# Eight experts, 67 MB of weights: float32 loads in the hardware queue and a cast on VectorE in place of casting loads from Pool

## The chip, the core and the metric

The kernel runs on one core of a Trainium2 chip. The core has five engines with queues of their own: TensorE (PE; PEld is its weight load), VectorE (DVE), ScalarE (ACT), GpSimd (POOL) and SyncE (SP), and 16 DMA engines that all of them share. The metric is device time in microseconds, the median of several runs, lower is better.

## What is computed

Eight independent experts, each with two matrix products and a ReLU between them. All arrays are float32.

```python
n_experts, capacity, hidden, expert_hidden = 8, 256, 512, 2048

def reference(x, w1, w2):          # x 8x256x512, w1 8x512x2048, w2 8x2048x512
    h = np.matmul(x, w1)
    h = np.maximum(h, 0)
    return np.matmul(h, w2).astype(np.float32)
```

Each of the 16 weight matrices has 4.194 MB (4 MiB) and is used once; x and the output have 4.194 MB each.

## The kernel before

Everything is multiplied in bf16 and accumulated in float32. x is loaded whole, 32 KB for each of 128 partitions, in two transfers (`HEAD`), cast to bf16 by VectorE and ScalarE, and transposed by TensorE into `xT`, in four rounds of 2 x 16 small matmuls, whose results VectorE and ScalarE copy out of PSUM (line 237).

Then a loop over the experts runs on TensorE. The first layer of an expert is 64 matmuls (`xT` against `w1_sb`), in two halves of two groups of 16; after each group ScalarE applies the ReLU and writes `hT` (line 279). The second layer is 32 matmuls (`hT` against `w2_sb`) into two PSUM banks `o_ps`, one for each 128 rows of output; VectorE copies both into `out_sb` (line 263), and for the last expert ScalarE copies the second one (line 285). All matmuls have line 315 in the profile, since one helper records them.

The weights come by casting DMAs that Pool issues (line 227): they read float32 from memory and write bf16 into one of `NS = 4` slots of `w1_sb` and `w2_sb`. The list `loads` sets their order: w1 and w2 of experts 0 and 1 together, then of 2 and 3, then w1 of 4 and 5, and from there mostly one matrix at a time; the last w2 is cut in two (`CUT`). Pool issues a load for a slot as soon as TensorE has read that slot's old contents, so several loads stand in its queue at any time. SyncE waits for the loads in the same order (line 179) and tells TensorE through the semaphores `c_w1` and `c_w2`; a whole w2 counts as two halves. SyncE's own queue carries x, the store of experts 0 to 6 in one transfer (line 174), issued when their outputs are in `out_sb`, and the store of expert 7 (line 186). The two queues feed the same 16 DMA engines.

Of the kernel before, what the change touches and what calls it, by code (L numbers as in the profile page):

```python
# [8 lines left out]
FP32 = mybir.dt.float32  # L9
BF16 = mybir.dt.bfloat16  # L10
# [6 lines left out]
def kernel(  # L17
# [7 lines left out]
    nc = tc.nc  # L25
    P = 128
# [7 lines left out]

    HEAD = 4

    NS = 4


    GJ = 4  # L40
    UG = 2
    NG = K2 // GJ

    JH = K2 // 2
    CUT = 11

    x_v = x.rearrange("e (pp r) k -> (e pp) (r k)", r=R)  # L50
    w1_v = w1.rearrange("e (p ko) n -> p e (ko n)", ko=K1)
    w2_v = w2.rearrange("e (p j) n -> p e j n", j=K2)
# [21 lines left out]
    x_sb = w2_sb[:, 2, :]  # L74
    X_AT = W2_AT + 2 * K2 * H * 2
# [14 lines left out]
    d_w = {  # L90
        (w, i): sem(f"d_w{w}_{i}")
        for w, slots in [(1, (0, 2, 3)), (2, (0, 1, 2, 3))]
        for i in slots
    }
    d_x, d_half = [sem(f"d_x{i}") for i in range(2)], sem("d_half")
    s_event, s_cast, s_stored = sem("s_event"), sem("s_cast"), sem("s_stored")
    s_pe, v_last = sem("s_pe"), sem("v_last")

    def take(engine, s, n):
        engine.wait_ge(s, n).then_inc(s, -n)  # L100
# [16 lines left out]

    loads = []  # L120
    for es in [(0, 1), (2, 3)]:
        loads += [(1, es, 0, 1), (2, es, 0, K2)]
    loads += [(1, (4, 5), 0, 1), (2, (4,), 0, K2), (2, (5,), 0, K2)]
    for e in range(6, E - 1):
        loads += [(1, (e,), 0, 1), (2, (e,), 0, K2)]
    loads += [(1, (E - 1,), 0, 1), (2, (E - 1,), 0, CUT), (2, (E - 1,), CUT, K2)]
    landed, counts = [], {}
    for w, es, a, _ in loads:
        s = d_half if a else d_w[w, es[0] % NS]
        counts[id(s)] = counts.get(id(s), 0) + 16  # L130
        landed.append((s, counts[id(s)]))

# [14 lines left out]

    sp = nc.sync

    def wide(a):  # L150
        rows, run = list(a.ap)
        return mybir.PhysicalAccessPattern(
            ap=[rows, [run[1], 1], run],
            offset=a.offset,
            dtype=a.dtype,
            memref=a.memref,
            memsetref=a.memsetref,
            dynamic_ap_info=a.dynamic_ap_info,
            shape_register=a.shape_register,
            bass_ap=a.bass_ap,  # L160
        )

    def copy_rows(dst, src):

        inst = mybir.InstDMACopy(
            name=nc.get_next_instruction_name(),
            engine=mybir.EngineType.SP,
            ins=[wide(a) for a in sp.lower_ap_dma(src)],
            outs=sp.lower_ap_dma(dst),
            mode="Copy",  # L170
            cce_op=mybir.AluOpType.bypass,
            queue="qSPDynamicHW",
        )
        return sp.add_instruction(inst)

    for i, (w, es, a, b) in enumerate(loads):
        sp.wait_ge(*landed[i])
        halves = 2 if b - a == K2 else 1
        sp.sem_inc((c_w1, c_w2)[w - 1], halves * len(es))
        if i == len(loads) - 2:  # L180
            sp.wait_ge(s_event, 3)
            copy_rows(
                out_v[:, :E - 1, :], out_sb[:, :E - 1].rearrange("p e m h -> p (e m h)")
            ).then_inc(d_last, 16)
    sp.wait_ge(v_last, MC)
    sp.dma_start(
# [4 lines left out]


    pool = nc.gpsimd

    def build_identity():
        pool.memset(identity[:], 0.0).then_inc(s_event)  # L196
        pool.wait_ge(s_event, 1)

        pool.affine_select(  # L199
            out=identity[:],  # L200
            in_=identity[:],
            compare_op=mybir.AluOpType.not_equal,
            fill=1.0,
            base=0,
            pattern=[[-1, P]],
            channel_multiplier=1,
        ).then_inc(s_event)

    for i, (w, es, a, b) in enumerate(loads):


        old = es[-1] - NS
        if w == 2 and 2 in es:
            build_identity()
            pool.wait_ge(*after_transposes(K1 * MC))
        if old >= 0 and a == 0:
            if w == 1:
                pool.wait_ge(*after_hidden(old, NG))
            else:
                pool.wait_ge(*after_outputs(old, MC))  # L220
        e, ne, at_slot = es[0], len(es), es[0] % NS
        if w == 2:
            src = w2_v[:, e:e + ne, a:b, :].rearrange("p e j n -> p e (j n)")
            dst = w2_sb[:, at_slot:at_slot + ne, a * H:b * H]
        else:
            src, dst = w1_v[:, e:e + ne, :], w1_sb[:, at_slot:at_slot + ne, :]
        pool.dma_start(dst, src).then_inc(landed[i][0], 16)  # L227
    pool.wait_ge(s_stored, 1)
    used = [s.num for s in sems[1:]]
    used = range(min(used), max(used) + 1)  # L230
# [9 lines left out]
        )  # L240


    dve = nc.vector
    SPLIT = 12

    def cast(copy, a, b):
        return copy(x_sb[:, rows(a, b)], x_f32[:, rows(a, b)])  # L247

    dve.wait_ge(d_x[0], 16)
    cast(dve.tensor_copy, 0, HEAD).then_inc(s_cast)  # L250
    dve.wait_ge(d_x[1], 16)
    cast(dve.tensor_copy, HEAD, SPLIT).then_inc(s_cast)
    dve.sem_inc(c_xt[0], 1)
    for ko in range(K1):
        dve.wait_ge(*after_transposes(ko * MC + 1))
        copy_xt(dve.tensor_copy, ko, 0).then_inc(c_xt[0])
    dve.sem_inc(c_o, MC)
    for e in range(E):
        for m in range(MC):
            if e == E - 1 and m == 1:  # L260
                break
            dve.wait_ge(*after_outputs(e, m + 1))
            cp = dve.tensor_copy(out_sb[:, e, m, :], o_ps[m][:])  # L263
            cp.then_inc(v_last if e == E - 1 else c_o)
        if e == E - 2:
            dve.drain().then_inc(s_event)


    act = nc.scalar
    act.wait_ge(d_x[1], 16)  # L270
    cast(act.copy, SPLIT, R).then_inc(s_cast)
    act.sem_inc(c_xt[1], 1)
    for ko in range(K1):
        act.wait_ge(*after_transposes(ko * MC + 2))
        copy_xt(act.copy, ko, 1).then_inc(c_xt[1])
    for e in range(E):
        for g in range(NG):
            act.wait_ge(*after_hidden(e, g + 1))
# [5 lines left out]
    act.wait_ge(*after_outputs(E - 1, MC))  # L284
    act.copy(out_sb[:, E - 1, 1, :], o_ps[1][:]).then_inc(v_last)  # L285

# [46 lines left out]
    def last_column(step):  # L333

        return (P - 1) * step * 2
# [5 lines left out]
    def transposes():  # L341
        i = 0
        for m in range(MC):
            take(pe, c_xt[m], 1)
            for r2 in range(R // MC):
                if i % 6 == 0:
                    for k in range(i, min(i + 6, n)):
                        row = (k % (R // MC)) * MC + k // (R // MC)
                        pe.reg_add(bank[i // 6 % 2][k - i], reg["x"], row * H * 2)
                    if i + 6 > n:  # L350
                        pe.reg_add(reg["x"], reg["x"], 2)
                t = matmul(
                    xt_ps[m][:, r2, :],
                    at(w2_sb, bank[i // 6 % 2][i % 6], [[K1, P]]),
                    pe.lower_ap(identity[:]),
                    start_tensor_calc=True,
                    stop_tensor_calc=True,
                    is_transpose=True,
                )
                i += 1  # L360
            t.then_inc(s_pe)

    pe.wait_ge(s_event, 2)
    pe.wait_ge(s_cast, 3)
    x_first = X_AT + last_column(K1)
    pe.reg_mov(reg["x"], x_first)
# [36 lines left out]
        compute(address1, range(a, b), regs)  # L403

    def set_expert():
        slot = reg["slot"]
        pe.reg_mod(slot, count, NS)
        pe.reg_mul(slot, slot, K1 * F * 2)
        pe.reg_add(reg["b1"], slot, W1_AT + last_column(K2))
        pe.reg_add(reg["b2"], slot, W2_AT)  # L410
        for ko in range(K1):
            pe.reg_add(reg[f"xt{ko}"], reg[f"xt{ko}"], P * 2)
        first_addresses()
# [100 lines left out]
```

## Time and profile before

| What | Value |
|---|---|
| median of 3 runs | 179.04 us (179.0 to 179.16) |
| the profiled execution | 179.38 us |
| its span, first to last instruction | 178.1 us |
| TensorE busy | 127.6 us, 72% |
| ScalarE busy | 40.6 us, 23% |
| VectorE busy | 18.1 us, 10% |
| Pool's DMA queue, share of 16 engines | 88.7% |
| SyncE's DMA queue, share of 16 engines | 11.3% |

An engine's busy time is what its instructions took; a DMA queue's share is the time of its packets against 16 engines over the span. The MB of a queue are the bytes it wrote, so a casting load of float32 into bf16 counts half of what it read. What stands outside the span (1.3 us of the profiled execution) is start and end of the program.

### The profile page before, as it was taken

The page shows a single profiled execution, that of the slowest core. Times are in us where ns is not written, and L with a number is a line of the kernel's source. Part 1 is how long each engine was busy: PE and PEld are TensorE (multiplying, and loading weights), DVE is VectorE, ACT ScalarE, POOL GpSimd, SP SyncE. Part 2 cuts the span into 40 slices and gives each one's busy share as a digit, 9 for nine tenths or more (in the row PEclk, how much of TensorE's full clock was granted, in tenths as well). Part 3 has the DMA queues.
Part 4 walks back from the last instruction along what each step waited for, and adds up shares of the span by engine and source line. Part 5 has one row for each costly group of instructions (what it writes and reads, how often), then busy time and mean ns, then how long its engine had stood idle before and what let it go on. Part 6 is the DMA issues. An engine that isn't in the chain of part 4 may idle for free. (4 is left out here: it accounts for less than half of the span.)

```text
span 178.1 us, 2074 instructions
## 1 busy us (share of the span) xinstructions
PE 127.6 (72%) x832; PEld 89.5 (50%) x832; DVE 18.1 (10%) x21; ACT 40.6 (23%) x39; POOL 9.2 (5%) x18
## 2 busy tenths in 40 slices
PE   0000066698039999994069999999999999969980
PEld 0000055587014695593023695596597498449530
DVE  0200435200000200200000200200020020020010
ACT  2000424226000053044000063044044036005310
POOL 3500000100000002101000101110000000000000
PEclk9999999999957999999756999999999999999996
DMA  6999999999999989989989999999999999999997
GB/s 212 431 294 300 236 213 199 236 217 195 236 202 210 236 177 236 232 180 236 232 180 236 232 195 221 232 202 213 236 202 210 236 210 202 236 198 202 336 412 324
DMA packets 2945, 41.94 MB, mean 236 GB/s; under 512 B 257, under 2 KB 257, under 8 KB 513
## 3 DMA queue, kind: packets, MB, share of 16 engines
q0 software_dynamic: 2368, 33.56, 88.7%
q1 hardware_dynamic: 576, 8.39, 11.3%
q14 instruction: 1, 0.00, 0.0%
HBM read 71.30 MB, written 4.19 MB: 424 GB/s over the span
## 5 line engine op out<-in xcount | busy, mean ns | idle before, releaser
L315 PE MATMUL o_ps<-w_sb,hT 128*128 x256 | 61.4, 402 | 16.8 <-PEq L100 16.8
L315 PE MATMUL h_ps<-xT,w_sb 128*128 x512 | 60.2, 279 | 3.2 <-PEq L100 3.2
L315 PEld LDWEIGHTS h_ps<-xT,w_sb 128*128 x512 | 57.3, 145 | 7.0 <-issue 3.9
L279 ACT ACTIVATE hT<-h_ps 128x1024 bf16<-128x1024 f32 x32 | 32.7, 1023 | 100.3 <-PE h_ps L315 100.3
L315 PEld LDWEIGHTS o_ps<-w_sb,hT 128*128 128x128 bf16 x256 | 25.6, 102 | 49.9 <-issue 23.8
L315 PE MATMUL xt_ps<-identity,w_sb 128*128 128x128 bf16 x64 | 7.6, 310 | 25.3 <-PEq L100 25.3
L263 DVE COPY out_sb<-o_ps 128x512 f32<-128x512 f32 x15 | 9.7, 686 | 130.4 <-PE o_ps L315 130.4
L315 PEld LDWEIGHTS xt_ps<-identity,w_sb 128*128 x64 | 6.5, 144 | 26.0 <-issue 26.0
L227 POOL DMA_DIRECT2D w_sb<-in_w_dram x12 | 7.4, 621 | 106.5 <-PE h_ps L315 47.5
L237 ACT COPY xT<-xt_ps 128x1024 bf16<-128x1024 bf16 x4 | 4.0, 1012 | 7.7 <-PE xt_ps L315 7.7
L247 ACT CAST w_sb<-out_sb 128x2048 bf16<-128x2048 f32 x1 | 1.9, 1898 | 16.5 <-DMA out_sb<-in_x_dram 16.5
L237 DVE COPY xT<-xt_ps 128x1024 bf16<-128x1024 bf16 x4 | 4.9, 1224 | 5.8 <-PE xt_ps L315 5.8
L247 DVE CAST w_sb<-out_sb 128x2048 bf16<-128x2048 f32 (+1 forms) x2 | 3.5, 1760 | 19.0 <-DMA out_sb<-in_x_dram 19.0
L285 ACT COPY out_sb<-o_ps 128x512 f32<-128x512 f32 x1 | 0.6, 585 | 5.9 <-PE o_ps L315 5.9
L247 ACT ACT_TABLE_LOAD x1 | 1.3, 1283 | 2.4 <-PEq L146 2.4
L199 POOL TENSOR_SCALAR_AFFINE_SELECT identity<-identity 128x128 bf16<-128x128 bf16 x1 | 1.4, 1375 | 0.2 <-POOL identity L196 0.2
L196 POOL MEMSET identity<- 128x128 bf16 x1 | 0.2, 231 | 0.0
L498 POOL MEMSET const-float32-0.0<- 128x1 f32 x1 | 0.1, 98 | 0.2 <-issue 0.2
L498 POOL MEMSET const-bfloat16-1.0<- 128x1 bf16 x1 | 0.1, 101 | 0.0
L498 POOL MEMSET const-uint8-127<- 128x1 uint8 x1 | 0.1, 101 | 0.0
L498 POOL MEMSET const-float32-1.0<- 128x1 f32 x1 | 0.1, 98 | 0.0
## 6 DMA issues: line engine op xcount, KB each, us to landing
w_sb<-in_w_dram POOLq DMA_DIRECT2D x5, 4096.0 KB, 47.8
w_sb<-in_w_dram POOLq DMA_DIRECT2D x5, 2048.0 KB, 50.7
out_dram<-out_sb SPq DMA_DIRECT2D x1, 3584.0 KB, 11.6
out_sb<-in_x_dram SPq DMA_DIRECT2D x1, 3072.0 KB, 19.0
w_sb<-in_w_dram POOLq DMA_DIRECT2D x1, 1408.0 KB, 50.0
out_sb<-in_x_dram SPq DMA_DIRECT2D x1, 1024.0 KB, 4.8
w_sb<-in_w_dram POOLq DMA_DIRECT2D x1, 640.0 KB, 52.5
out_dram<-out_sb SPq DMA_DIRECT2D x1, 512.0 KB, 4.5
```

What stands on the lines that cost most here:

```text
L196: pool.memset(identity[:], 0.0).then_inc(s_event)
L199: pool.affine_select(out=identity[:], in_=identity[:], compare_op=mybir.AluOpType.not_equal, fill=1.0, base=0, pattern=[[-1, P]], channel_ ...
L227: pool.dma_start(dst, src).then_inc(landed[i][0], 16)
L237: return copy(xT[:, ko, m].rearrange("k (ep r2) -> k ep r2", r2=R // MC), xt_ps[m][:].rearrange("k r2 ep -> k ep r2"),)
L247: return copy(x_sb[:, rows(a, b)], x_f32[:, rows(a, b)])
L263: cp = dve.tensor_copy(out_sb[:, e, m, :], o_ps[m][:])
L279: act.activation(hT[:, g * GJ:(g + 1) * GJ, :].rearrange("p a c -> p (a c)"), h_ps[g % UG][:], mybir.ActivationFunctionType.Relu,).then_in ...
L285: act.copy(out_sb[:, E - 1, 1, :], o_ps[1][:]).then_inc(v_last)
L315: return pe.add_instruction(inst)
L498: nc = _bacc.Bacc("TRN2", target_bir_lowering=False, num_devices=1)
```

## The change

All loads go through SyncE's hardware queue, in float32, into a staging buffer `stage` with two places: one for w1, one for w2. VectorE casts from there into a single bf16 copy, `w1_sb` or `w2_sb`. A w1 is cast in one instruction of 8192 columns, a w2 in two of 4096. SyncE issues w1 and w2 of expert 0 right behind x; after that, a matrix of the next expert is issued when the cast of the same matrix of this expert is done, so that at most one transfer stands behind the running one. VectorE starts a cast when the load has landed and TensorE has read the old bf16 copy. The output copies and the xT copies that VectorE made move to ScalarE, except one of the last expert.

For the last expert w1 comes in two transfers (three quarters and one quarter), and ScalarE casts about a third of it beside VectorE; w2 comes in two halves. The store of experts 0 to 6 stands in the same queue behind the last load. Pool is left with the identity matrix. The order on TensorE stays as it was; only its address arithmetic loses the slots, since there is one copy to read.

```diff
-    NS = 4
+    NS = 2
...
-    w1_sb = allot("w1_sb", [P, NS, K1 * F], BF16)
-    w2_sb = allot("w2_sb", [P, NS, K2 * H], BF16)
+    stage = allot("stage", [P, NS, K1 * F], FP32)
+    w1_sb = allot("w1_sb", [P, K1 * F], BF16)
+    w2_sb = allot("w2_sb", [P, K2 * H], BF16)
...
+    KEEP = K1 - 1
+    LATE = F // 8 * 5
...
+    issue_all(1, 0)
+    issue_all(2, 0)
+    for i, (w, e, a, b) in enumerate(loads):
+        for k in range(len(casts[i])):
+            sp.wait_ge(s_weights, last_cast[i] - len(casts[i]) + k + 1)
+            if w == 2 or b == K1 * F:
+                sp.sem_inc((c_w1, c_w2)[w - 1], 1)
+        if b == K1 * F:
+            issue_all(w, e + 1)
+        if (w, e) == (1, E - 1) and b == K1 * F:
+            sp.wait_ge(s_out, 1)
+            copy(
...
+    for i, (w, e, a, b) in enumerate(loads):
+        dve.wait_ge(*landed[i])
+        if a == 0:
+            if (w, e) == (2, 0):
+                dve.wait_ge(*after_transposes(K1 * MC))
+            if e > 0:
+                dve.wait_ge(*(after_hidden(e - 1, NG) if w == 1 else after_outputs(e - 1, MC)))
+        helped = w == 1 and e == E - 1
+        for a, b in casts[i]:
+            if helped:
+                b = b - F if b < K1 * F else a + LATE
+                cast_w(dve.tensor_copy, i, a, b)
+                dve.wait_ge(s_helped, 1 if a == 0 else 2)
+                dve.drain().then_inc(s_weights)
+            else:
+                cast_w(dve.tensor_copy, i, a, b).then_inc(s_weights)
...
+        if e == E - 2:
+            for i, (w, e1, a, b) in enumerate(loads):
+                if (w, e1) == (1, E - 1):
+                    act.wait_ge(*landed[i])
+                    if a == 0:
+                        act.wait_ge(*after_hidden(e, NG))
+                    cast_w(act.copy, i, b - F if a == 0 else a + LATE, b).then_inc(s_helped)
+        for m in range(MC):
+            act.wait_ge(*after_outputs(e, m + 1))
+            if e < E - 1:
+                act.copy(out_sb[:, e, m, :], o_ps[m][:]).then_inc(c_o)
```

SyncE's queue before, the whole of it. The first two rows load x, the last two store the output; the waits of the store name the loads' semaphores, since SyncE passes their landings on to TensorE first.

```order
L143 DMA out_sb_55<-in_x_dram 128x2048
L143 DMA out_sb_55<-in_x_dram 128x6144
L146 UNCONDITIONAL_BRANCH
L174 DMA out_0_dram<-out_sb_55 128x7x1024 [waits barrier_Pool_Activation_PE_DVE_SP_release,d_w1_0,d_w2_0,d_w1_2,d_w2_2,d_w2_1,d_w1_3,d_w2_3,s_event]
L186 DMA out_0_dram<-out_sb_55 128x1024 [waits d_half,v_last]
```

SyncE's queue of the change, its start: x, the two first weight loads, and the first refill of each place (`s_weights` counts the casts).

```order
L140 DMA out_sb_55<-in_x_dram 128x2048
L140 DMA out_sb_55<-in_x_dram 128x6144
L143 UNCONDITIONAL_BRANCH
L176 DMA stage_56<-in_w1_dram 128x8192 [waits barrier_Pool_Activation_PE_DVE_SP_release]
L176 DMA stage_56<-in_w2_dram 128x8192
L176 DMA stage_56<-in_w1_dram 128x8192 [waits s_weights]
L176 DMA stage_56<-in_w2_dram 128x8192 [waits s_weights]
```

The sixteen matrices, which Pool's queue carried, stand here behind x, and each refill waits for a cast. The end of the same queue of the change, from the last w1 on:

```order
L176 DMA stage_56<-in_w1_dram 128x6144 [waits s_weights]
L176 DMA stage_56<-in_w1_dram 128x2048
L176 DMA stage_56<-in_w2_dram 128x4096 [waits s_weights]
L176 DMA stage_56<-in_w2_dram 128x4096
L157 DMA out_0_dram<-out_sb_55 128x7x1024 [waits s_weights,s_out]
L213 DMA out_0_dram<-out_sb_55 128x1024 [waits s_weights,v_last]
```

The store of seven experts, which had a queue without loads, now follows the last load in the same one. VectorE before, from the casts of x on (`s_pe` counts TensorE's groups of work):

```order
L247 CAST w2_sb_57<-out_sb_55 128x2048 [waits barrier_Pool_Activation_PE_DVE_SP_release,d_x0]
L247 CAST w2_sb_57<-out_sb_55 128x4096 [waits d_x1]
L237 COPY xT_58<-xt_ps0 128x1024 [waits s_pe] x4
L263 COPY out_sb_55<-o_ps0 128x512 [waits s_pe]
L263 COPY out_sb_55<-o_ps1 128x512 [waits s_pe]
```

VectorE of the change, the same stretch (`d_w0` and `d_w1` are the landings in the two places of `stage`):

```order
L251 CAST w2_sb_58<-out_sb_55 128x2048 [waits barrier_Pool_Activation_PE_DVE_SP_release,d_x0]
L251 CAST w2_sb_58<-out_sb_55 128x4096 [waits d_x1]
L255 CAST w1_sb_57<-stage_56 128x8192 [waits d_w0]
L255 CAST w2_sb_58<-stage_56 128x4096 [waits s_pe,d_w1]
L255 CAST w2_sb_58<-stage_56 128x4096
L255 CAST w1_sb_57<-stage_56 128x8192 [waits s_pe,d_w0]
```

The copies have left VectorE, and the casts stand in their place, one w1 and two halves of w2 for each expert.

## Rows read from the trace of the kernel before

**Rows 1.** The page, busy us, share of the span and instructions.

```profile
PE 127.6 (72%) x832; PEld 89.5 (50%) x832; DVE 18.1 (10%) x21; ACT 40.6 (23%) x39; POOL 9.2 (5%) x18
```

**Rows 2.** The page, DMA queues: packets, MB, share of 16 engines.

```profile
q0 software_dynamic: 2368, 33.56, 88.7%
q1 hardware_dynamic: 576, 8.39, 11.3%
...
HBM read 71.30 MB, written 4.19 MB: 424 GB/s over the span
```

**Rows 3.** Busy time by stretch; last: clock, DMA share, GB/s written.

```profile
core 0: us, PE busy (x) PEld busy (x) DVE busy (x) ACT busy (x) POOL busy (x), PEclk, DMA share, GB/s
1.50:2.60 1.10, 0.00 (x0) 0.00 (x0) 0.00 (x0) 0.21 (x1) 0.00 (x0) 1.00 0.84 179
...
2.60:7.40 4.80, 0.00 (x0) 0.00 (x0) 1.23 (x1) 1.07 (x1) 3.85 (x5) 1.00 1.01 427
...
36.00:70.00 34.00, 26.02 (x166) 18.50 (x164) 1.29 (x2) 8.18 (x8) 1.28 (x2) 0.90 1.02 216
70.00:124.00 54.00, 45.18 (x289) 30.95 (x288) 3.86 (x6) 12.28 (x12) 3.19 (x6) 0.91 1.02 218
...
124.00:166.00 42.00, 40.51 (x281) 29.37 (x280) 3.86 (x6) 11.33 (x12) 0.00 (x0) 1.00 1.00 212
```

**Rows 4.** DMA queues from 2.6 to 7.4 us: packets, MB, share.

```profile
q1 hardware_dynamic: 168, 2.03, 99.8%
```

**Rows 5.** DMA queues from 70 to 124 us.

```profile
q0 software_dynamic: 783, 11.78, 102.3%
```

**Rows 6.** TensorE in time: start us, us, what, idle before and releaser.

```profile
90.79 9.99 PE L315 MATMUL o_ps<-w_sb,hT 128*128 x32 [8.82 <-PEq L100]
...
150.02 7.07 PE L315 MATMUL o_ps<-w_sb,hT 128*128 x32
...
158.57 7.32 PE L315 MATMUL h_ps<-xT,w_sb 128*128 x64 [1.49 <-PEq L100]
```

**Rows 7.** SyncE's waits for loads: duration in ns, first and last start in us.

```profile
L179 SPq EVENT_SEMAPHORE  x12: 17/17/17, 32.2 to 168.2; - x12
```

**Rows 8.** The end in time: stores and the last output copy.

```profile
165.21 0.64 SPq L174 DMA_DIRECT2D out_dram<-out_sb  x1
...
172.88 0.58 ACT L285 COPY out_sb<-o_ps 128x512 f32<-128x512 f32 x1 [5.93 <-PE o_ps L315]
173.49 0.35 SPq L186 DMA_DIRECT2D out_dram<-out_sb  x1
```

**Rows 9.** DMA issues: count, KB each, median us from issue to landing.

```profile
w_sb<-in_w_dram POOLq DMA_DIRECT2D x5, 4096.0 KB, 47.8
...
out_dram<-out_sb SPq DMA_DIRECT2D x1, 3584.0 KB, 11.6
...
out_dram<-out_sb SPq DMA_DIRECT2D x1, 512.0 KB, 4.5
```

**Rows 10.** The start in time: x, its casts, the first transposes.

```profile
0.74 0.85 SPq L143 DMA_DIRECT2D out_sb<-in_x_dram  x2
...
5.59 1.23 DVE L247 CAST w_sb<-out_sb 128x2048 bf16<-128x2048 f32 x1 [5.59 <-DMA out_sb<-in_x_dram]
...
20.21 2.29 DVE L247 CAST w_sb<-out_sb 128x4096 bf16<-128x4096 f32 x1 [13.39 <-DMA out_sb<-in_x_dram]
...
23.06 1.89 PE L315 MATMUL xt_ps<-identity,w_sb 128*128 128x128 bf16 x16 [23.06 <-PEq L100]
```

**Rows 11.** Copies by form: busy us, mean ns, idle before.

```profile
L263 DVE COPY out_sb<-o_ps 128x512 f32<-128x512 f32 x15 | 9.7, 686 | 130.4 <-PE o_ps L315 130.4
...
L237 ACT COPY xT<-xt_ps 128x1024 bf16<-128x1024 bf16 x4 | 4.0, 1012 | 7.7 <-PE xt_ps L315 7.7
...
L285 ACT COPY out_sb<-o_ps 128x512 f32<-128x512 f32 x1 | 0.6, 585 | 5.9 <-PE o_ps L315 5.9
```

**Rows 12.** The stretch behind the idle time of 8.82 us, columns as in rows 3.

```profile
86.50:93.00 6.50, 2.21 (x6) 0.85 (x7) 0.00 (x0) 0.00 (x0) 0.00 (x0) 0.50 0.96 204
```

More of the change, by code (lines that the diff above doesn't have):

```diff
@@ L88 @@
     d_last = sem("d_last")
[L90 to L97, printed above, removed]
+    d_x = [sem(f"d_x{i}") for i in range(2)]
+    d_w = [sem(f"d_w{i}") for i in range(NS)]
+    d_rest = [sem(f"d_rest{i}") for i in range(2)]
+    s_identity, s_cast, s_stored = sem("s_identity"), sem("s_cast"), sem("s_stored")
+    s_weights, s_helped = sem("s_weights"), sem("s_helped")
+    s_pe, s_out, v_last = sem("s_pe"), sem("s_out"), sem("v_last")
     def take(engine, s, n):
@@ L115, with slot @@
     c_xt = [sem("c_xt"), c_h]
+    KEEP = K1 - 1
+    LATE = F // 8 * 5
     loads = []
[L121 to L126, printed above, removed]
+    for e in range(E):
+        last = e == E - 1
+        for w, parts in [
+            (1, [(0, KEEP * F), (KEEP * F, K1 * F)] if last else [(0, K1 * F)]),
+            (2, [(0, JH * H), (JH * H, K2 * H)] if last else [(0, K2 * H)]),
+        ]:
+            loads += [(w, e, a, b) for a, b in parts]
+    def slot(w, e):
+        return w - 1
     landed, counts = [], {}
-    for w, es, a, _ in loads:
-        s = d_half if a else d_w[w, es[0] % NS]
+    for w, e, a, b in loads:
+        s = d_rest[w - 1] if a else d_w[slot(w, e)]
         counts[id(s)] = counts.get(id(s), 0) + 16
@@ L148, with copy, pattern @@
     sp = nc.sync
-    def wide(a):
-        rows, run = list(a.ap)
+    def copy(dst, src):
+        inst = mybir.InstDMACopy(
+            name=nc.get_next_instruction_name(),
+            engine=mybir.EngineType.SP,
+            ins=[src],
+            outs=[dst],
+            mode="Copy",
+            cce_op=mybir.AluOpType.bypass,
+            queue="qSPDynamicHW",
+        )
+        return sp.add_instruction(inst)
+    def pattern(ap, dims):
+        (a,) = sp.lower_ap_dma(ap)
         return mybir.PhysicalAccessPattern(
-            ap=[rows, [run[1], 1], run],
+            ap=dims,
             offset=a.offset,
@@ L161, in wide, with issue, issue_all @@
         )
[L163 to L183, printed above, removed]
+    def issue(i):
+        w, e, a, b = loads[i]
+        src = (w1_v, w2_v)[w - 1][e]
+        dst = stage[:, slot(w, e), :]
+        sp.dma_start(dst[:, a:b], src[:, a:b]).then_inc(landed[i][0], 16)
+    casts, last_cast = [], []
+    for i, (w, e, a, b) in enumerate(loads):
+        if w == 1:
+            parts = [(a, b)]
+        else:
+            parts = [(c, c + JH * H) for c in range(a, b, JH * H)]
+        casts.append(parts)
+        last_cast.append((last_cast[-1] if last_cast else 0) + len(parts))
+    def issue_all(w, e):
+        for i, load in enumerate(loads):
+            if load[:2] == (w, e):
+                issue(i)
+    issue_all(1, 0)
[10 more added lines that the diff above has]
+            copy(
+                pattern(out_v[:, :E - 1, :], [[MC * H, P], [C * H, E - 1], [1, MC * H]]),
+                pattern(
+                    out_sb[:, :E - 1].rearrange("p e m h -> p (e m h)"),
+                    [[E * MC * H, P], [(E - 1) * MC * H, 1], [1, (E - 1) * MC * H]],
+                ),
             ).then_inc(d_last, 16)
@@ L193 @@
     pool = nc.gpsimd
[L195 to L227, printed above, removed]
+    pool.memset(identity[:], 0.0).then_inc(s_identity)
+    pool.wait_ge(s_identity, 1)
+    pool.affine_select(
+        out=identity[:],
+        in_=identity[:],
+        compare_op=mybir.AluOpType.not_equal,
+        fill=1.0,
+        base=0,
+        pattern=[[-1, P]],
+        channel_multiplier=1,
+    ).then_inc(s_identity)
     pool.wait_ge(s_stored, 1)
@@ L240, in copy_xt, with cast_x, cast_w @@
         )
-    dve = nc.vector
+    dve, act = nc.vector, nc.scalar
     SPLIT = 12
-    def cast(copy, a, b):
+    def cast_x(copy, a, b):
         return copy(x_sb[:, rows(a, b)], x_f32[:, rows(a, b)])
+    def cast_w(copy, i, a, b):
+        w, e = loads[i][:2]
+        return copy((w1_sb, w2_sb)[w - 1][:, a:b], stage[:, slot(w, e), a:b])
     dve.wait_ge(d_x[0], 16)
-    cast(dve.tensor_copy, 0, HEAD).then_inc(s_cast)
+    cast_x(dve.tensor_copy, 0, HEAD).then_inc(s_cast)
     dve.wait_ge(d_x[1], 16)
-    cast(dve.tensor_copy, HEAD, SPLIT).then_inc(s_cast)
@@ L253 @@
-    dve.sem_inc(c_xt[0], 1)
+    cast_x(dve.tensor_copy, HEAD, SPLIT).then_inc(s_cast)
+    for i, (w, e, a, b) in enumerate(loads):
+        dve.wait_ge(*landed[i])
[11 more added lines that the diff above has]
+                dve.drain().then_inc(s_weights)
+            else:
+                cast_w(dve.tensor_copy, i, a, b).then_inc(s_weights)
@@ L254 @@
+    dve.wait_ge(*after_outputs(E - 1, 1))
+    dve.tensor_copy(out_sb[:, E - 1, 0, :], o_ps[0][:]).then_inc(v_last)
+    act.wait_ge(d_x[1], 16)
+    cast_x(act.copy, SPLIT, R).then_inc(s_cast)
+    for m in range(MC):
+        act.sem_inc(c_xt[m], 1)
     for ko in range(K1):
[L255 to L258, printed above, removed]
         for m in range(MC):
[L260 to L266, printed above, removed]
@@ L269 @@
[L269 to L275, printed above, removed]
+            act.wait_ge(*after_transposes(ko * MC + m + 1))
+            copy_xt(act.copy, ko, m).then_inc(c_xt[m])
+    act.sem_inc(c_o, MC)
     for e in range(E):
@@ L353, in transposes @@
                     xt_ps[m][:, r2, :],
-                    at(w2_sb, bank[i // 6 % 2][i % 6], [[K1, P]]),
+                    at(x_sb, bank[i // 6 % 2][i % 6], [[K1, P]]),
                     pe.lower_ap(identity[:]),
@@ L361, in transposes @@
             t.then_inc(s_pe)
-    pe.wait_ge(s_event, 2)
+    pe.wait_ge(s_identity, 2)
     pe.wait_ge(s_cast, 3)
@@ L405, in set_expert @@
     def set_expert():
[L406 to L410, printed above, removed]
+        pe.reg_add(reg["b1"], reg["b1"], -JH * 2 * 2)
         for ko in range(K1):
```

15 lines of the change are left out of this document (8 added, 7 removed).

## The prediction

> **What bounds the kernel now.** I read the busy lines first. TensorE works 127.6 us of a span of 178.1 us, VectorE 18.1, ScalarE 40.6 [rows 1]; none of them fills the span. The table of DMA queues says what does: the Pool queue's packets take 88.7% of the time of all 16 DMA engines and the SyncE queue's 11.3%, which is 100.0% together [rows 2]. The casting transfers show 33.56 MB because the page counts bytes written; they read twice that, and HBM read is 71.30 MB. The DMA share by stretch confirms it: 1.00 to 1.02 from 2.6 to 166 us [rows 3]. The chain of waits names only TensorE's last two layers (8% of the span) and not the DMA. I don't take it for the bound: those layers run beside the end of the loads and the store of the first seven experts.
>
> Then the rate. TensorE waited for a load at 90.79 us (second layer of expert 2, the load of experts 2 and 3) and next in the loads' order at 158.57 us (first layer of expert 7) [rows 6]. Between these landings lie seven experts' matrices of 4.194 MB of float32 (one double load and five single ones): 67.78 / 7 = **9.68 us each**, 433 GB/s read. All loads had landed at 168.2 us, when SyncE's last wait on one ended [rows 7]. The store of seven experts, issued at 165.21, landed 11.6 us later, at 176.8, which is 8.6 us after the last load; the last store landed 1.2 us behind it, at 173.49 + 4.5 = 178.0 [rows 8, 9]. So the time is the time in which 71.3 MB is read and 4.2 MB written, and an edit pays only if it changes that stream or its ends.
>
> **The change part by part.** *The loads' bytes.* 67.1 MB of weights is still read, in float32 as before. What doubles is what is written into SBUF: 67.1 instead of 33.56 MB. Is the stream paced by what it reads or by what it writes? The trace of before has one uncovered stretch of the plain form: 2.6 to 7.4 us, x alone in the SyncE queue, 427 GB/s written and read, at 99.8% of the engines' time [rows 3, 4]. The casting form, from 70 to 124 us, writes 218 and so reads 436 GB/s at 102.3% [rows 3, 5]. Per unit of engine time that is 428 against 426 GB/s of reading: equal. Reading paces both, and the doubled writing is free. A float32 load of 4.194 MB therefore takes between 9.68 us (landing to landing, above) and 4.194 / 0.427 = 9.82 us. I take **9.68**, because the stretch at 427 holds the start-up's stragglers: from 1.5 to 2.6 us the queue still ran at 179 GB/s [rows 3].
>
> *The loads' order.* Before, x shares the engines with the first weights and lands only at 20.2 us, where VectorE's second cast starts [rows 10]. Now x stands first in the one queue and the first weights follow. From 1.5 to 2.6 us 0.20 MB moves; the other 4.00 MB at 427 GB/s ends at 12.0. Sixteen loads of 9.68 us are 154.9: bytes end at 166.9. The landing comes about 1.0 us later: the first part of x (1.05 MB) should by these rates be moved at 4.6 us, and VectorE started on it at 5.59 [rows 10]. **Last landing 167.9**, against 168.2 before. At 9.82 us per load it is 170.1.
>
> *Does the queue ever run dry?* Each buffer is refilled only when its cast is done, so one load is always queued behind the running one, if cast and issue take less than a load. The cast of 8192 columns isn't in the trace: 2048 columns took 1.23 and 4096 took 2.29 us [rows 10], so 0.52 ns a column and 0.17 fixed, 4.4 us. I give 0.5 us for the way through SyncE (the x cast ended at 22.50 and TensorE started at 23.06 [rows 10]), and 0.8 us from issue to first bytes (the issue stands at 0.74 [rows 10]; the stretch from 1.5 us has bytes [rows 3]). Together 5.7 of 9.68 us: 3.9 us of cover, and it hides the whole of 16 casts, some 71 us of VectorE time that before didn't have. If VectorE ran one column per cycle as from PSUM (512 columns in 686 ns [rows 11], with a like fixed part some 1.0 ns a column), the cast would take 8.4 us, the sum 9.7, and the cover is gone.
>
> The casts also wait for TensorE to have read the one bf16 copy. With w1 of an expert landing at t, the first layer starts at t + 4.9 and ends at t + 12.2 (7.32 us [rows 6]); the second (7.07 us [rows 6]) starts at t + 12.5, when the first half of w2 (landed t + 9.7) is cast, and ends at t + 19.5. Nothing that waits for either layer is needed before t + 19.4 (next w1) or t + 29 (next w2, which waits for the second layer): 7 and 9.5 us of cover.
>
> *ScalarE* takes over 4 xT copies (1.01 us each) and 14 output copies (0.585 us) from VectorE [rows 11]: some 12 us, spread over the span. All eight xT copies on it end between 24 us (8 x 1.01 behind the cast of x, which ends near 15.3) and 31 (each behind its own transposes, 0.95 us); the first w1 is cast near 27. Even 31 delays only a first layer that has 7 us of cover. Near the end ScalarE also casts a third of the last w1, and expert 6's output copies stand behind these casts: they run at T - 8.9 (T is the last landing), and the first who needs them is TensorE in the middle of expert 7's first layer, near T - 4.8. *Pool's* twelve issues go and nobody had waited for that engine: nothing. On SyncE each refill stands behind the wait for its cast, and behind nothing else.
>
> *The end.* From the last landing T = 167.9: half of w2 is cast (2.29 us), 0.5 for the way, half of a second layer (3.54), then 0.61 from ScalarE's last copy to the issue of the last store (172.88 to 173.49 [rows 8]): T + 6.9 = 174.8, first bytes 175.6. Before, that issue came at 173.49, so the end of the work moves back 1.3 us. It stays covered: the seven experts' store follows the last load in the queue and lands at T + 8.6 = 176.5, its last bytes near 176.0, and the last store lands 1.2 us later, **177.7**. The cover is some 0.4 us and thin.
>
> Sum: 177.7 against 178.0 is -0.3 us of span. The profiled execution took 179.38 us, 1.3 more than its span; the median of the runs is 179.04, and to this I apply the difference: 178.75, rounded **178.8 us**. Its own range, from 0.5 us to either side for start and landing lags: 178.3 to 179.3. A difference of 0.2% (0.36 us) is about what a measurement of this kernel can tell from none.
>
> **The rivals.**
> *Plain loads run at 427 GB/s.* 16 x 0.14 = 2.2 us more: 181.0. For it speaks that the only plain row says so; against it, that its engine share is 99.8% where the casting form shows 102.3%. Slower from 9.71 us per load on.
> [...]
> *Software descriptors had held the stream back.* From 36 to 70 us the rate was 216 and from 124 to 166 us 212 instead of 218 GB/s [rows 3]: 34 x 2/218 + 42 x 6/218 = 1.5 us, if all of it came from the Pool queue and the new one has none: 177.3. Against it: the landing-to-landing time of 9.68 us already spans 124 to 158. [...]
> *Each load pays its own start.* If a transfer in one queue began only behind the landing of the one before, each would lose about 1.8 us (0.8 to first bytes, 1.0 landing lag): 16 x 1.8 = 29 us, 208. Against it: the stretch at 99.8% holds the seam between the two transfers of x. [...] A cast that outlasts its cover goes with this case: at 9.7 us for cast, way and start each of 14 refills would just come late, and each further 0.3 us costs 4: 183.
>
> **How the numbers follow.** Forecast 0.48 (0.12 of it below 178.7, 0.34 within 0.2%, 0.02 above); slower plain loads 0.17, up to 181.0, of which 0.04 stays within 0.2%; late last layers 0.13, of which 0.04 stays within; smoother stream 0.15, down to 177.3, all of it faster; queue dry or transfers with a start of their own 0.07. Faster 0.27, same 0.42, slower 0.31. The range runs from 177.9 (half of the smoother case is below) to 181.2 (beyond the 427 GB/s case).
>
> **What would show it.** Right: casts of w1 near 4.4 us; DMA share about 1.0 from 2.6 us to the end with no dip between loads; w1 landings 19.4 us apart (the starts of the first layers too); the last store's landing some 1.2 us behind the other's. Wrong: landings 19.6 us apart or more; share under 0.95 in the middle; a DMA gap between the two stores, which would say that TensorE became the end.

## The result and the profile after

The changed kernel takes **180.84 us** (median of 4 runs, 180.75 to 180.95) against 179.02 (4 runs, 178.98 to 179.16): ratio **1.0101, interval 1.0083 to 1.0118**. It is 1.8 us slower. The forecast was 178.8, no change; the time lies inside the range (177.9 to 181.2), the direction was missed. The profiled execution took 180.93 us, its span is 179.6.

From the page after: busy times, then the DMA queues (packets, MB, share of 16 engines).

```profile
PE 132.2 (74%) x832; PEld 92.3 (51%) x832; DVE 74.4 (41%) x28; ACT 54.4 (30%) x59; POOL 0.7 (0%) x6
...
q1 hardware_dynamic: 3168, 75.50, 98.2%
q8 instruction: 1, 0.02, 0.0%
q14 instruction: 1, 0.01, 0.0%
HBM read 71.30 MB, written 4.19 MB: 420 GB/s over the span
```

One queue carries everything, at 98.2%. Two lines count packets of kind "instruction", 0.02 and 0.01 MB. The page before has only this one:

```profile
q14 instruction: 1, 0.00, 0.0%
```

The new line, q8, looks like nothing, and it is most of this case.

VectorE in time after (start us, us, what, idle before and its releaser). Each cast starts when its load has landed (the last landed at 169.79 and its cast started at 169.81), so the starts are the landings.

```profile
12.87 2.29 DVE L251 CAST w_sb<-out_sb 128x4096 bf16<-128x4096 f32 x1 [6.04 <-DMA out_sb<-in_x_dram]
22.58 4.43 DVE L255 CAST w_sb<-stage 128x8192 bf16<-128x8192 f32 x1 [7.42 <-DMA stage<-in_w_dram]
32.30 4.50 DVE L255 CAST w_sb<-stage 128x4096 bf16<-128x4096 f32 x2 [5.29 <-DMA stage<-in_w_dram]
...
80.86 4.43 DVE L255 CAST w_sb<-stage 128x8192 bf16<-128x8192 f32 x1 [5.22 <-DMA stage<-in_w_dram]
91.97 4.50 DVE L255 CAST w_sb<-stage 128x4096 bf16<-128x4096 f32 x2 [6.68 <-DMA stage<-in_w_dram]
101.69 4.43 DVE L255 CAST w_sb<-stage 128x8192 bf16<-128x8192 f32 x1 [5.22 <-DMA stage<-in_w_dram]
...
169.81 2.29 DVE L255 CAST w_sb<-stage 128x4096 bf16<-128x4096 f32 x1 [2.59 <-DMA stage<-in_w_dram]
```

Whole loads land 9.7 us apart (9.69 to 9.72), except one: from 80.86 to 91.97 there are 11.11 us, and the idle time is 6.68 instead of 5.2 to 5.3. The 1.4 us are never made up; the last landing is at 169.8. The DMA queues after from 82 to 86 us:

```profile
q1 hardware_dynamic: 49, 1.61, 93.9%
q8 instruction: 1, 0.02, 1.7%
```

A block of 16 KB of instructions starts at 82.67 us and holds one of the 16 DMA engines for 1.07 us (1.7% of 16 x 4 us). The data packet that starts as it ends, at 83.72, takes 1.71 us; those of the loads before took 1.21 to 1.22. The trace has 16 landings for each load. From the first to the last of them, the **lag**, it is 0.55 us in the load that landed at 80.84, 1.94 in the next, the last one alone 1.40 behind the fifteen others, and still 1.76 in the last load. So one part in sixteen of every later load is late, and a cast waits for the last part of its load (91.95 us, its cast at 91.97). That the late part is always that of the engine which carried the block fits these landings, but isn't shown: the trace neither numbers the engines nor says which partitions one of them fills.

The end in time after, and SyncE's last issue:

```profile
161.09 7.36 PE L344 MATMUL h_ps<-xT,w_sb 128*128 x64 [1.30 <-PEq L89]
168.34 3.61 PE L344 MATMUL o_ps<-w_sb,hT 128*128 x16
172.29 3.61 PE L344 MATMUL o_ps<-w_sb,hT 128*128 x16 [0.33 <-PEq L89]
175.99 0.59 ACT L313 COPY out_sb<-o_ps 128x512 f32<-128x512 f32 x1 [6.48 <-PE o_ps L344]
176.60 0.35 SPq L213 DMA_DIRECT2D out_dram<-out_sb  x1
```

Beside [rows 8] the last store is issued 3.1 us later (176.60 against 173.49). But the span ends about as long behind the last landing in both kernels: 9.8 us (179.6 - 169.8) and 9.9 (178.1 - 168.2). So the loss lies ahead of the last landing, in the stream of loads.

### The profile page after: what moved, and what is told of

Read it like the earlier page. It is cut to its first block, busy times and chain, and to the rows that moved or that the text cites. A ratio compares the mean times of both kernels' runs of the same rounds, so it can differ in the third digit from the quotient of the medians.

```text
span 179.6 us, 2130 instructions
## 1 busy us (share of the span) xinstructions
PE 132.2 (74%) x832; PEld 92.3 (51%) x832; DVE 74.4 (41%) x28; ACT 54.4 (30%) x59; POOL 0.7 (0%) x6
## 3 DMA queue, kind: packets, MB, share of 16 engines
q1 hardware_dynamic: 3168, 75.50, 98.2%
## 5 line engine op out<-in xcount | busy, mean ns | idle before, releaser
L255 DVE CAST w_sb<-stage 128x4096 bf16<-128x4096 f32 (+2 forms) x25 | 70.2, 2830 | 86.8 <-DMA stage<-in_w_dram 81.5
L344 PE MATMUL h_ps<-xT,w_sb 128*128 x512 | 69.0, 303 | 25.8 <-PEq L89 25.8
L344 PEld LDWEIGHTS h_ps<-xT,w_sb 128*128 x512 | 61.7, 149 | 34.9 <-issue 30.0
L344 PE MATMUL o_ps<-w_sb,hT 128*128 x256 | 56.7, 379 | 0.6 <-PEq L89 0.6
L344 PEld LDWEIGHTS o_ps<-w_sb,hT 128*128 128x128 bf16 x256 | 24.4, 97 | 30.1 <-issue 1.4
L311 ACT COPY out_sb<-o_ps 128x512 f32<-128x512 f32 x14 | 7.5, 588 | 34.4 <-PE o_ps L344 34.4
L241 ACT COPY xT<-xt_ps 128x1024 bf16<-128x1024 bf16 x8 | 7.7, 1015 | 3.5 <-PE xt_ps L344 3.5
L255 ACT CAST w_sb<-stage 128x2048 bf16<-128x2048 f32 (+1 forms) x2 | 2.7, 1366 | 4.6 <-DMA stage<-in_w_dram 4.6
L313 ACT COPY out_sb<-o_ps 128x512 f32<-128x512 f32 x1 | 0.6, 586 | 6.5 <-PE o_ps L344 6.5
L280 DVE COPY out_sb<-o_ps 128x512 f32<-128x512 f32 x1 | 0.7, 691 | 3.6 <-PE o_ps L344 3.6
L223 POOL TENSOR_SCALAR_AFFINE_SELECT identity<-identity 128x128 bf16<-128x128 bf16 x1 | 0.3, 292 | 0.2 <-POOL identity L221 0.2
```

Of the source, the lines that this page charges most:

```text
L223: pool.affine_select(out=identity[:], in_=identity[:], compare_op=mybir.AluOpType.not_equal, fill=1.0, base=0, pattern=[[-1, P]], channel_ ...
L241: return copy(xT[:, ko, m].rearrange("k (ep r2) -> k ep r2", r2=R // MC), xt_ps[m][:].rearrange("k r2 ep -> k ep r2"),)
L255: return copy((w1_sb, w2_sb)[w - 1][:, a:b], stage[:, slot(w, e), a:b])
L280: dve.tensor_copy(out_sb[:, E - 1, 0, :], o_ps[0][:]).then_inc(v_last)
L311: act.copy(out_sb[:, e, m, :], o_ps[m][:]).then_inc(c_o)
L313: act.copy(out_sb[:, e, m, :], o_ps[m][:]).then_inc(v_last)
```

## The experiments

Two theories. **Block**: the 16 KB of instructions that pass through one DMA engine cost the time. **Casts**: the stream is held by what the change put behind each load (VectorE's casts, their writes into SBUF, refills that are issued too late for the seam between two loads). Each run stands beside the kernel before on the same chip; the ratios are against that.

### Whose block is it?

In `act_merged` ScalarE's two output copies of an expert are one instruction, so ScalarE has fewer instructions:

```diff
-        for m in range(MC):
-            act.wait_ge(*after_outputs(e, m + 1))
-            if e < E - 1:
-                act.copy(out_sb[:, e, m, :], o_ps[m][:]).then_inc(c_o)
...
+        act.wait_ge(*after_outputs(e, MC))
+        if e < E - 1:
+            act.copy(out_sb[:, e], o_both[:]).then_inc(c_o)
...
```

> The changed kernel with ScalarE's two output copies of an expert merged into one of 128x1024 (65 instructions on ScalarE in place of 73; TensorE then waits for them once per expert, before its second layer). Theory A, the lag: at 82.7 us one DMA engine carries a 16 KB block of instructions beside its weights, falls 1.4 us behind and stays behind, since each engine has its own partitions. If ScalarE fetched that block (A1), the block is gone here, the 11.1 us step between two cast starts becomes 9.7, the last cast starts at 168.4 instead of 169.8, and the time is 179.4 us. If SyncE or VectorE fetched it (A2), or if the step has another cause (rival B: the plain float32 stream is slow by itself), it stays at 180.8.

Measured: 180.79 us, 1.0103 (1.0086 to 1.0119). The 16 KB block is still there, at 81.25 us.

In `w2_whole` each w2 but the last is cast in one instruction, so VectorE and SyncE have fewer:

```diff
-        if w == 1:
+        if w == 1 or e < E - 1:
             parts = [(a, b)]
...
```

> The changed kernel with each w2 but the last cast in one instruction of 8192 columns (46 instructions on VectorE in place of 53, 50 on SyncE in place of 57; second layers start 2.2 us later, which is covered). A2 (SyncE or VectorE fetched the block): no block, 179.4 us. A1 or B: the step stays, 180.8 us.

Measured: 180.95 us (180.69 to 182.19), 1.0108 (1.0091 to 1.0125); the block is there, at 82.45. The longest execution, 182.19, is the profiled one; what sets it apart from the rest lies at its end and is told below, with the late layers.

`before_actpad` and `before_sppad` go the other way: the kernel before with 30 empty increments of a semaphore on ScalarE, or 32 on SyncE.

```diff
...
+    for _ in range(30):
+        act.sem_inc(s_pad, 1)
```

> The kernel before with 30 empty semaphore increments on ScalarE, behind its xT copies, where it waits for TensorE for 4 us anyway (78 instructions in place of 48). A1: a 16 KB instruction packet appears in mid-run, one DMA engine falls 1.1 to 1.4 us behind to the end, time 180.1 to 180.4 us. A2 and B: 179.0 us.

> The kernel before with 32 empty semaphore increments on SyncE just ahead of the wait for the last outputs, where it is idle (59 instructions in place of 27). A2 with SyncE as the fetcher: a 16 KB instruction packet in mid-run and 180.1 to 180.4 us. A1 and B: 179.0 us.

Measured: 179.05 us, 1.0003 (0.9994 to 1.0013), and 179.14, 1.0009 (0.9999 to 1.0019). ScalarE's padding brings a block of 8 KB into a kernel that had none, at 47.3 us and without a lasting lag; SyncE's brings nothing. All this speaks against these three engines as the ones that fetch the 16 KB, though VectorE was only shortened and not padded. In the three kernels that had it, the block began 0.2 to 0.5 us ahead of the end of expert 2's second layer, whatever else had moved; that pointed to TensorE's own stream.

### TensorE's instructions

`pe_pad1` adds one empty increment to TensorE's loop over the experts (by the change the loop's body had lost one: 40 in place of 41 behind the inner loop), `pe_pad8` adds eight, and `before_pe8` adds eight to the kernel before.

```diff
...
+                for _ in range(1):
+                    pe.sem_inc(s_pad, 1)
```

> The changed kernel with one empty semaphore increment more in TensorE's loop over the experts, which gives its body the length it had before (41 instructions behind the inner loop, not 40). The block of 16 KB came 0.24 to 0.53 us ahead of the end of the third second layer in all three kernels that had it, wherever that end stood, so TensorE's own stream is now the suspect (theory A3). If the block depends on the body's length, it is gone, the last cast starts at 168.4 and the time is 179.4 us. If it only depends on something else in this kernel, or if the loss has another cause (B), 180.8.

> The same with eight increments per expert. A3: the block is gone (179.4 us) or stands at another expert, since TensorE reaches a given count of instructions earlier; a block that comes earlier costs the same 1.4 us (180.8). If it stays ahead of the end of the third second layer, TensorE's instruction count doesn't place it.

> The kernel before with eight empty increments per expert on TensorE. A3: a block of 16 KB may appear here too, and if so one DMA engine lags by 1.1 to 1.4 us to the end and the time is 180.1 to 180.4 us. Without a block: 179.0 us.

Measured: `pe_pad1` **179.87 us**, 1.0045 (1.0031 to 1.0059); `pe_pad8` 180.71, 1.0091 (1.0074 to 1.0108); `before_pe8` 179.98, 1.0053 (1.0037 to 1.0070). VectorE in time, `pe_pad1`:

```profile
80.85 4.43 DVE L256 CAST w_sb<-stage 128x8192 bf16<-128x8192 f32 x1 [5.22 <-DMA stage<-in_w_dram]
90.56 4.50 DVE L256 CAST w_sb<-stage 128x4096 bf16<-128x4096 f32 x2 [5.28 <-DMA stage<-in_w_dram]
...
168.75 2.29 DVE L256 CAST w_sb<-stage 128x4096 bf16<-128x4096 f32 x1 [2.59 <-DMA stage<-in_w_dram]
```

The same view of `pe_pad8`:

```profile
61.43 4.43 DVE L256 CAST w_sb<-stage 128x8192 bf16<-128x8192 f32 x1 [5.22 <-DMA stage<-in_w_dram]
72.28 4.50 DVE L256 CAST w_sb<-stage 128x4096 bf16<-128x4096 f32 x2 [6.42 <-DMA stage<-in_w_dram]
81.99 4.43 DVE L256 CAST w_sb<-stage 128x8192 bf16<-128x8192 f32 x1 [5.21 <-DMA stage<-in_w_dram]
```

And the DMA queues of `before_pe8` from 75 to 79 us:

```profile
q0 software_dynamic: 59, 0.97, 113.4%
q8 instruction: 1, 0.02, 1.5%
```

One instruction more, and the 16 KB block and the long step are gone. Eight more, and the block comes one expert, that is two loads, earlier (62.97 us), with a long step of 10.85 us there. In the kernel before, which had no block, eight instructions bring one (76.25 us): the lag grows from 0.50 to 1.24 us, the last landing comes at 168.5, and the time is 0.9 us longer. So the block goes with TensorE's program, and it costs time in either kernel: the landing behind it is 0.7 to 1.4 us late in the kernels that have one. Why one instruction more keeps it away, these runs don't tell.

`pe_pad1` gains 0.97 us of the block's 1.4, because a second block shows up: the page's 8 KB (q14). In the kernel after, it fell at 156.3 us and left the lag as it was (1.81 us ahead of it, 1.77 behind); in `pe_pad1`, at 157.2, it lengthens the lag from 0.50 to 0.87 us.

### Casts?

`short_cast`: VectorE casts only the first 512 columns of each piece, except for experts 0 and 7; the rest of these weights is left out.

```diff
-                cast_w(dve.tensor_copy, i, a, b).then_inc(s_weights)
+                cast_w(dve.tensor_copy, i, a, b if e in (0, E - 1) else a + H).then_inc(s_weights)
```

> The changed kernel with VectorE casting only the first 512 columns of each piece for experts 1 to 6 (the rest of the weights is left out, so the bf16 copy there is that of expert 0); all loads, matmuls and copies run. Refills are issued some 4 us earlier. If casts or late refills slow the stream (rival C), loads come 9.68 us apart in place of 9.715 and without the engines' pauses at the seams, and the last cast starts 0.5 us earlier or more: 180.3 or less, with the block still there. If only the block costs (A), the time is 180.6 to 180.8.

Measured: 181.08 us, 1.0113 (1.0096 to 1.0129). VectorE in time:

```profile
61.38 0.43 DVE L255 CAST w_sb<-stage 128x512 bf16<-128x512 f32 x1 [8.95 <-DMA stage<-in_w_dram]
71.10 0.76 DVE L255 CAST w_sb<-stage 128x512 bf16<-128x512 f32 x2 [9.29 <-DMA stage<-in_w_dram]
81.97 0.43 DVE L255 CAST w_sb<-stage 128x512 bf16<-128x512 f32 x1 [10.11 <-DMA stage<-in_w_dram]
91.68 0.76 DVE L255 CAST w_sb<-stage 128x512 bf16<-128x512 f32 x2 [9.28 <-DMA stage<-in_w_dram]
```

With casts of 0.43 us in place of 4.43 the refills are issued up to 4 us earlier (expert 2's w1 at 42.48 instead of 46.52), but the landings are 9.71 us apart as before, and the block's long step stands (10.87 us, to 81.97). The theory of the casts falls: neither their work nor the time at which a refill is issued sets the pace. The run also speaks for TensorE once more. Its loop is that of the kernel after, but expert 2's second layer ends 4.1 us earlier, at 78.78, and the block has gone along: it starts at 78.73 instead of 82.67.

### What is left without blocks

`lean` is `pe_pad1` with fewer instructions on ScalarE: VectorE casts the last w1 alone and takes back one output copy of each expert, and three counter increments go to Pool.

```diff
...
+            cast_w(dve.tensor_copy, i, a, b).then_inc(s_weights)
+        if w == 1 and e > 0 and b == K1 * F:
+            dve.wait_ge(*after_outputs(e - 1, 1))
+            dve.tensor_copy(out_sb[:, e - 1, 0, :], o_ps[0][:]).then_inc(c_o)
...
```

> The changed kernel without either block of instructions: the increment of pe_pad1 on TensorE, and ScalarE's program shortened from 73 to 59 instructions (VectorE makes one of the two output copies of each expert, behind the cast of the next w1, and casts the last w1 alone; three empty increments go from ScalarE to Pool). An 8 KB block at 156 to 158 us appeared in all runs with 65 or more instructions on ScalarE from which it was absent with 48, and in pe_pad1 one DMA engine fell 0.34 us behind there. Theory A (blocks on one DMA engine are the loss): no block from 1 us on, the 16 engines land each load within 0.6 us of each other to the end, last cast at 168.3 to 168.5 us, time 179.4 to 179.5. Rival B (the float32 stream is what costs): 179.8 as pe_pad1 or more.

> The lean kernel once more, beside the next run on the same chip. Both theories: 179.6 to 179.7 (ratio 1.003 to 1.004), TensorE's last 96 matmuls without a gap from 160.8 to 175.1 us, last store issued near 175.7.

The place that this names for the 8 KB block is too narrow: in the runs of the changed kernel so far it stood at 154.3 to 165.9 us.

Measured: **179.66 us**, 1.0035 (1.0021 to 1.0049), and once more 179.78, 1.0043 (1.0029 to 1.0056). The instruction line of its page is down to 0.00 MB:

```profile
q14 instruction: 1, 0.00, 0.0%
```

VectorE's second landing and the end of `lean` in time:

```profile
32.26 4.49 DVE L259 CAST w_sb<-stage 128x4096 bf16<-128x4096 f32 x2 [5.29 <-DMA stage<-in_w_dram]
...
160.78 7.32 PE L333 MATMUL h_ps<-xT,w_sb 128*128 x64 [1.27 <-PEq L90]
...
167.99 7.07 PE L333 MATMUL o_ps<-w_sb,hT 128*128 x32
...
168.40 2.29 DVE L259 CAST w_sb<-stage 128x4096 bf16<-128x4096 f32 x1 [2.61 <-DMA stage<-in_w_dram]
...
175.71 0.35 SPq L214 DMA_DIRECT2D out_dram<-out_sb  x1
```

The last landing is now 168.4, 1.4 us ahead of the kernel after. Yet `lean` is still 0.7 us behind the kernel before, more than the traces so far show (168.4 against 168.2). Its end has changed too: TensorE goes without a gap from 160.78 to 175.06 and no longer waits for the last cast. So three kernels shorten that end.

`lean_tail` cuts the last w2 at 11/16, so that its last cast is shorter:

```diff
...
-            (2, [(0, JH * H), (JH * H, K2 * H)] if last else [(0, K2 * H)]),
+            (2, [(0, 11 * H), (11 * H, K2 * H)] if last else [(0, K2 * H)]),
...
```

> lean with the last w2 cut at 11 of 16 parts in place of 8, so that what is cast behind the last landing is 2560 columns and not 4096 (1.5 us in place of 2.3). The last store is issued some 0.75 us earlier. If the end hangs on the work behind the last landing (the store finds the engines idle), the time falls by up to 0.7 us against lean, to about 178.8; if the other store still covers it, it stays within 0.2 us of lean.

`lean_early` brings the last w1 in three transfers, so that TensorE starts sooner; `lean_early3` also moves three output copies from ScalarE to VectorE.

```diff
...
-            (1, [(0, KEEP * F), (KEEP * F, K1 * F)] if last else [(0, K1 * F)]),
+            (1, [(0, 2 * F), (2 * F, 7 * F // 2), (7 * F // 2, K1 * F)] if last else [(0, K1 * F)]),
...
```

> Lean, with the last w1 in three transfers (a half, three eighths, one eighth) in place of two (three quarters, a quarter), so that VectorE is done with it sooner. Theory A (what is left against before is the end: the last store is issued after the big store has drained, near 176.1 us, and its first bytes come 1.2 us after its issue): expert 7's first layer starts near 159.9 instead of 160.8, the last store is issued near 174.9 to 175.0, its bytes follow the big store's without a gap, span 177.9 to 178.1, time 179.2 to 179.4. Theory B (what is left is the stream of loads itself, so the last landing): the issue moves as in A but the time stays within 0.1 us of the lean kernel's, 179.6 to 179.7.

> The lean kernel with the last w1 in three transfers, and three more output copies moved from ScalarE to VectorE (ScalarE six instructions fewer, VectorE six more). Theory A (the 0.45 us that the three transfers added outside the span came from a block of instructions that was fetched behind the end of the work): no such block, 1.3 us outside the span, span 178.2, time 179.5 to 179.6. Theory B (it came from something else in the form of three transfers): still 1.8 to 2.0 us outside the span, time 180.0 to 180.3.

Measured: `lean_tail` 179.94 us, 1.0053 (1.0039 to 1.0067), with a span of 178.3 as `lean` (178.4), since that cast was not waited for. `lean_early` 180.24, 1.0068 (1.0055 to 1.0082); `lean_early3` 179.82, 1.0047 (1.0033 to 1.0060). `lean_early` at the end:

```profile
159.88 7.31 PE L333 MATMUL h_ps<-xT,w_sb 128*128 x64 [0.52 <-PEq L90]
...
175.07 0.35 SPq L214 DMA_DIRECT2D out_dram<-out_sb  x1
```

The last store in the DMA issues from 166 to 180 us (KB, us from issue to landing), of `lean_again` and then of `lean_early`:

```profile
out_dram<-out_sb SPq DMA_DIRECT2D x1, 512.0 KB, 2.6
```

```profile
out_dram<-out_sb SPq DMA_DIRECT2D x1, 512.0 KB, 3.1
```

The issue comes 0.6 us earlier (175.07 against 175.65), as expected, but the landing only some 0.1: 175.65 + 2.6 against 175.07 + 3.1. That fits a store which waits for the big store ahead of it and so covers the end of the work; little was to be had there: the span is 178.2 against 178.3. And the time grows, outside the span: 1.8 to 2.0 us instead of 1.3 in `lean`. The page of `lean_early` has a block of 8 KB again, fetched at 179.9 us, when the work is done. In `lean_tail`, 0.3 us above `lean`, such a block stands at 180.05 in the profiled execution, which had 2.0 us outside its span (1.4 to 2.0 in the others); in `lean_early3` at 177.6, with 1.6 us outside its span. The expectation for the last was no block and 179.5, or 180.0 and more; it is neither. That a block near the end lengthens the program fits these kernels; whose it is, and that it is the cause, isn't settled.

Then the kernel before once more, unchanged, since its first trace was 0.36 us above the median of its runs:

> The kernel before, unchanged, for a second trace of it: the first one (179.38 us, span 178.1) lay 0.36 us above the median of its runs, so the row by row comparison lacks that much. All theories: 179.0, ratio 1.000. If the profiled execution comes out at a span of 177.6 to 177.9, its last wait for a load tells where the 0.4 us lie: near 167.8 (then the stream of loads in the changed kernel ends 0.5 us later than before's, and the rest is the stream) or still 168.2 (then it is the end).

Measured: 178.96 us, 0.9998 (0.9989 to 1.0007), span 177.6. SyncE's waits for loads, columns as in [rows 7]:

```profile
L179 SPq EVENT_SEMAPHORE  x12: 17/17/17, 32.1 to 167.7; - x12
```

Its end in time:

```profile
158.12 7.31 PE L315 MATMUL h_ps<-xT,w_sb 128*128 x64 [2.10 <-PEq L100]
...
173.04 0.35 SPq L186 DMA_DIRECT2D out_dram<-out_sb  x1
```

This settles the rest. The last landing is at **167.7** here, 0.5 us earlier than in the first trace, and the end behind it is as long (9.9 us). By the landings themselves (the waits and casts shown start 0.02 us behind them), 14 loads take from 32.12 to 167.69 here: 135.57 us, **9.68** each. In `lean` the same 14 take from 32.24 to 168.38: 136.14 us, **9.72** each. So 0.7 us lie in the landing (0.6 of it in the pace of the loads), and 0.1 in the end (178.4 - 168.4 = 10.0).

| kernel | time | last landing | span end behind it |
|---|---|---|---|
| before (second trace) | 178.96 | 167.7 | 9.9 |
| `lean`, no blocks | 179.66 | 168.4 | 10.0 |
| after | 180.84 | 169.8 | 9.8 |

So of the 1.8 us, 1.2 go with the blocks (180.84 against 179.66 in `lean`), and 0.6 to 0.7 are left without them.

The way from 9.68 to 9.72 is open in its cause, but the landings in the traces say where it lies. Before, thirteen whole loads took 9.68 us each, and the last w2, in two transfers, 9.74. In `lean` twelve whole loads took 9.71 each, and the last two matrices, in four transfers, 19.59 together. So 0.4 us come from whole loads, and under 0.2 from the pieces at the end. Of the kernel after, the first three landings behind x are 9.71, 9.72 and 9.71 us apart at the casts, and short casts don't change it. Whether the doubled writing, the other queue or the other packets make the 0.03 us a load, no run here separates. No kernel here is faster than the one before.

## Why the forecast missed

**Right: the bound.** The span ended 9.8 to 10.0 us behind the last landing in every profiled execution but one (`w2_whole`, below). TensorE's 132.2 and VectorE's 74.4 us of work did not matter.

**Right, but for a small rest: reading paces, the doubled writing is free.** At 9.71 us a load, the float32 form is 0.3% from the casting form (9.68), with twice the bytes written. The rival of plain loads at 427 GB/s named 181.0, close to the time; that is luck, since the pace is 9.71 and not 9.82. But its mark, "slower from 9.71 us per load on", was just met: without the blocks `lean` is still 0.7 us behind.

**Right: x first, and the queue never dry.** x's second cast started at 12.87 (bytes at 12.0 and a landing 1.0 later were forecast). The cast of 8192 columns took 4.43 us against 4.4 from two rows. The first refill was issued at 27.10, 0.1 us behind the cast's end, where 0.5 was allowed. Transfers with a start of their own, and a dry queue, fall: no landing came late but behind the block.

**Late last layers, 0.13 in the chances: none that held up the end of this kernel.** TensorE in time after, and below it the same two layers by stretch, columns as in [rows 3]:

```profile
66.05 9.91 PE L344 MATMUL h_ps<-xT,w_sb 128*128 x64 [3.62 <-PEq L89]
...
145.14 7.35 PE L344 MATMUL h_ps<-xT,w_sb 128*128 x64 [3.60 <-PEq L89]
```

```profile
66.05:75.96 9.91, 9.91 (x65) 8.53 (x66) 4.50 (x2) 3.07 (x3) 0.00 (x0) 0.72 0.98 423
...
145.14:152.49 7.35, 7.35 (x64) 6.93 (x64) 2.24 (x2) 3.07 (x3) 0.00 (x0) 1.00 0.96 414
```

First layers of experts 0 to 5 took 8.8 to 9.9 us instead of 7.3, behind idle times of 2.6 to 4.8 us. Expert 2's had a granted clock of 0.72 in the mean (0.50 up to 71.70 us, 1.00 from there on) and expert 6's 1.00, behind idle times of nearly the same length (3.62 and 3.60 us). Expert 6's ran in 7.35, and nobody waited for the others.

In the profiled execution of `w2_whole` a late layer did hold up the end. Expert 6's second layer, in time and by stretch:

```profile
154.63 8.75 PE L344 MATMUL o_ps<-w_sb,hT 128*128 x31 [2.35 <-PEq L89]
```

```profile
154.63:163.38 8.75, 8.70 (x33) 3.77 (x35) 3.12 (x2) 2.91 (x3) 0.00 (x0) 0.80 0.98 413
```

Behind an idle time of 2.35 us it had a granted clock of 0.80 and took 8.75 us, against 1.00 and 7.07 us in the kernel after. Expert 7's first layer started at 163.22 instead of 161.09, the last store was issued at 178.20, and the span ended 11.3 us behind the last landing. This execution took 182.19 us where the median of its kernel is 180.95. In that kernel, whose second layers start later, the end can set the time.

**Wrong: "Last landing 167.9".** It came at 169.8. Of the 1.9 us, 1.4 are the 16 KB block, which no term of the sum held: the sum counted the bytes of data and took the 16 engines as one. The other 0.5 are the size of one term: sixteen loads at **9.68**, the pace of the casting form between two of TensorE's waits [rows 6], against 9.72 in `lean`, which has no block. That is 0.7 us, less some 0.2 by which x landed sooner than forecast. The bounds given, 9.68 to 9.82, held it. The sign "w1 landings 19.4 us apart" was met all the same, but for the one step with the block.

**Wrong: "to this I apply the difference".** The change was costed at -0.3 us against a profiled execution, and that was taken off the median. But the second trace of before shows that the first one's excess over the median was in the loads (168.2 against 167.7), a stretch that my sum built anew from rates and so did not contain. The forecast of 177.7 should have stood against 177.6, the end of the second trace, and not against 178.0: the same steps would have given about 179.1, a little slower instead of a little faster.

**Wrong, at no price: "It stays covered".** The last store was issued 6.8 us behind the last landing (6.9 forecast) and its first bytes moved 0.85 us later (0.8), at 177.45. But the last landing is that of one late engine: the others had drained the big store between 176.2 and 177.0 and stood idle. The late one was busy with it to 177.9, so the end stayed as long as forecast, 9.8 us.

**Not borne out: the rival of a smoother stream.** With no transfers left in Pool's queue, nothing was gained; before's own loads ran at 9.68.

## What to carry over

In this kernel, whose transfers fill the 16 DMA engines (98.2% of their time), 16 KB of instructions on one of them made the last landing 1.4 us later. In a profile of this kind look in the table of DMA queues for lines of kind "instruction", and at the starts of the waiting engine for one step that is longer than the others. Where a row of a profile is to be changed by a difference, ask first in which term that execution departs from the median, and whether the new sum contains it.

## What the hardware showed

A block of 16 KB of instructions came in the middle of the run, on one DMA engine, in 0.95 to 1.07 us. From there on one of the 16 parts of every load landed late, to the end: the lag grew by 0.7 us (`before_pe8`) to 1.4 us (the kernel after). The place moved with the length of TensorE's loop (62.97 us with eight instructions more, 82.67 as changed, none with one more) and with TensorE's progress (78.73 in `short_cast`). TensorE's layer beside it shows no loss (the second layer of expert 2, to 82.91 us, took 7.07 us as those of the other experts did), the loads do: 1.4 us of the last landing. Blocks of 8 KB also occurred (0.3 to 0.5 us on one engine); ahead of the last landing, only that of `pe_pad1` lengthened the lag (0.50 to 0.87 us).
